# Hybrid neighbourhood-attention and short-convolution block: the two score banks of PSUM as two tiles outside the attention, and DRAM scratch split by head and pair

## The chip, the cores and the metric

The kernel runs on one core of one Trainium2 chip. Its time is the device time of one execution, in microseconds (us), lower is better. Five engines work side by side, each through its own instructions in order: TensorE (PE, with the weight loads listed apart as PEld), VectorE (DVE), ScalarE (ACT), GpSimd (POOL) and SyncE (SP, which here only issues DMAs). An engine waits on semaphores that other engines or DMA queues raise.

## The reference

One layer on a latent sequence of 1024 tokens (16 rows of 64), width 1024, with 256 context tokens. All arithmetic is in float32.

```
h  = rmsnorm(x, norm_g)   * (1 + scale)   + shift      # adaLN from silu(c) @ w_ada + b_ada
hc = rmsnorm(ctx, norm_g) * (1 + scale_c) + shift_c
q, k, v, za, u, bg, cg, zc = split(h @ w_in)           # each 512 wide
kc, vc = split(hc @ w_in[:, 512:1536])
q, k, kc = rmsnorm of each head (8 heads of 64)
s_lat = rope(q) . rope(k) * 64**-0.5 + rpb             # window of 8 x 16 of the grid
s_ctx = q . kc * 64**-0.5                              # all 256 context keys
attn  = softmax([s_lat, s_ctx]) @ [v, vc] * silu(za)
conv  = bg * conv3(cg * u) * silu(zc)
x_new = x + gate * (concat([attn, conv]) @ w_out)
```

## The kernel before

**Arithmetic.** To keep float32 accuracy every operand of a large product is split into a high part (rounded) and a low part (the rest): `wh`, `wl` for weights, `hh`, `hl` for the normalised input h, `qs`, `ks`, `vs` for q, k and v. A product is three matmuls, high x high, high x low and low x high (`mm3`). A split is a copy on ACT (the high part) and a subtraction on DVE (the low part), `halves` and `chunk_split` in the code.

**Stages.** By the span's time: the setup (modulation, norm, tables; to about 85 us), the projections of q, k and v (85 to 306), the attention (306 to about 640), and the output projection. In the setup and in the attention the order of instructions on each engine is the order of the program text (`strict`). In the projections and the output a scheduler of the compiler orders them by its own estimates of time.

**Projections.** A loop over n has 32 tiles, 4 pairs of heads with 8 tiles (t = 0 to 7) of 128 tokens each. `proj_tile` computes one tile's q, k and v of a pair: 8 steps k (128 rows of the weights each) of three matmuls with 384 columns, 24 matmuls into one bank of PSUM. In the same pass the loop works on the tiles before it:

- `head_scale`: ACT squares tile n-1 (`sq`), DVE sums by head (`ss`), POOL takes the power -1/2;
- `put_v`: ACT and DVE split v out of the bank (`vs`);
- `normed`: ACT scales q and k of tile n-2 (`qn`, four activations);
- `rotated`: DVE applies the rotary table (`rtmp`, `rot`);
- `turn_qk`: PE transposes two tiles (`trA`, `trB`), ACT and DVE split them (`qs`, `ks`), SP stores them to `q_d`, `k_d`;
- after tile 2 of a pair (tile 0 of the last pair) `ctx_products` makes the context's k and v in two banks `cacc` (48 matmuls); their `sq`, `kn`, `vs` and transposes (`trC`, two of them) follow one to three tiles later;
- in pair 1 the gate row of the modulation is summed by two matmuls (`pgate`) and copied by ACT (`gr`);
- in the first tiles and the last ones, units of the convolution and gates (`pu`) fill in; their weights are loaded as `uraw` and split into `uh`, `ul`.

The weights of the next pair are loaded in chunks (`wr`), 8 for a pair, and split into `wh` and `wl`, each of which has a ring of 12 buffers: the last four splits of a pair can start only when the running pair's matmuls have let go of the first buffers.

**PSUM.** It has 8 banks of [128, 512] float32. The pool `psm` has three tags with two buffers each: O, C and U. The tag S is something else, one tile `sbank` of two banks from which `bank` hands out the halves in turn:

```
    sbank = psm.tile([P, 2, 512], F32, name="pss")          # line 854
    ...
    def bank(name, tag):                                    # line 857
        if tag != "S":
            return psm.tile([P, 512], F32, name=name, tag=tag, bufs=2)
        turns[0] += 1
        return sbank[:, turns[0] % 2]
```

Tile t of a pair takes the bank `"OOSS"[t % 4]`: t = 0, 1, 4, 5 write O banks (named `pacc` in the profile), t = 2, 3, 6, 7 write S halves (named `pss`). In the attention PE writes two tiles of scores into the two halves, and DVE adds the bias to both in one instruction, so that there the two halves are read as one. The output projection takes S, C and O banks for its first six tiles, and then U and S in turn.

The compiler's framework (Tile) tracks who wrote and who read by tile: an instruction that reads a tile waits for the instructions ahead of it in the program that wrote that tile.

**DRAM scratch.** q, k, v and the context's kc and vc go through scratch in DRAM (`q_d`, `k_d`, `v_d`, `kc_d`, `vc_d`), one tensor each with the head as its first index. So do the tables of biases (`t4_d`), the sums of the softmax (`rs_d`, `ri_d`), the attention's output (`o_d`), the gates (`zs_d`) and their products (`y_d`).

**SP's queue.** SP issues nearly all transfers in one order: chunk loads, `uraw`, the stores (collected in `stores` and issued by `flush` a tile later), and at the end of the projections the first heads' loads of the attention, `k_s`, `q_s`, `kc_s` and `v` (`load_k`, `load_q`, `load_v`). A store waits in the queue until the engine that makes its data is done, and all behind it wait too.

Of the kernel before, what the change touches and what calls it, by code (L numbers as in the profile page):

```python
# [10 lines left out]
F32 = mybir.dt.float32  # L11
# [8 lines left out]
P = 128  # L20
D = 1024
T = 1024
L = 256
# [16 lines left out]
def body(tc, es, x, ctxt, w_ada, b_ada, w_in, q_g, k_g, rpbr, w_out, vecs, cst, out):  # L40
# [45 lines left out]


    dr = es.enter_context(tc.tile_pool(name="dr", bufs=1, space=DRAM))
    t2_d = dr.tile([8, NH * 31, 24], F32, name="t2_d")
    t3_d = dr.tile([NH, 16, 8, 384], F32, name="t3_d")  # L90
    t4_d = dr.tile([NH, P, 3 * 384], F32, name="t4_d")
    o_d = dr.tile([NPAIR, P, T], F32, name="o_d")
    y_d = dr.tile([KT, P, T], F32, name="y_d")
    g_d = dr.tile([1, D], F32, name="g_d")
    rope_d = dr.tile([P, 2048], F32, name="rope_d")
    rs_d = dr.tile([NH, 2, 512], F32, name="rs_d")
    zs_d = dr.tile([NPAIR, P, T], F32, name="zs_d")


    q_d = dr.tile([NH, 2, HD, 4, 2, 256], F32, name="q_d")  # L100
    k_d = dr.tile([NH, HD, 4, 2, 256], F32, name="k_d")
    v_d = dr.tile([NH, P, 4, 2, 2 * HD], F32, name="v_d")
    kc_d = dr.tile([NH, HD, 2, L], F32, name="kc_d")
    vc_d = dr.tile([NH, P, 2, 2 * HD], F32, name="vc_d")
    ri_d = dr.tile([NPAIR, 2, T], F32, name="ri_d")


    cp = es.enter_context(sbuf("cp"))
# [83 lines left out]
    def spill(dst, src):  # L192
        stores.append(lambda: sp.dma_start(dst, src.bitcast(F32)))
# [21 lines left out]
    def turn_qk(pp, p, two, t0):  # L215

        pA = psm.tile([P, 2, 2, P], F32, name="trA", tag="C", bufs=2)
        pB = psm.tile([P, 512], F32, name="trB", tag="C", bufs=2)
        for i, (qn, rot) in enumerate(two):
            pe.transpose(pA[:, 0, i], rot[:, 0:P], ident)  # L220
            pe.transpose(pA[:, 1, i], qn[:, 0:P], ident)
            pe.transpose(pB[:, i * P:(i + 1) * P], rot[:, P:256], ident)

        def put():
            qs = pp.tile([P, 2, 2, 256], F32R, name="qs", tag="qs", bufs=2)
            halves(qs[:, 0], qs[:, 1], pA[:].rearrange("p k i d -> p k (i d)"))
# [146 lines left out]
    def conv_group(i, done=None):  # L373
# [55 lines left out]
        def times(half, v, last):  # L429
            dve.tensor_tensor(by_row(cvs[half][:]), blocked(v), by_row(cvs[half][:]), ALU.mult)  # L430
            if last:
                sp.dma_start(y_d[4 + i, :, half * 512:(half + 1) * 512], cvs[half])

        def gains():
            for half, ps in sorted(done[CBG].items()) if done else ():
# [37 lines left out]
    def attn_group(f):  # L473

        z = []
        for got in unit(z_col(f)):
            if got:
                z.append(got)
            else:
                yield  # L480

        def on_act():
            for half, zs in enumerate(silus(z)):
                sp.dma_start(zs_d[f, :, half * 512:(half + 1) * 512], zs)
        chore(on_act)

    def recip(p, pl):

        ri = pl.tile([P, 16], F32, name="ri", tag="ri", bufs=2)
        pool.dma_start(ri, rs_d[2 * p:2 * p + 2].rearrange("h b (x c) -> (h b x) c", c=16))  # L490
        dve.reciprocal(ri, ri)
        pool.dma_start(ri_d[p].rearrange("h (x c) -> (h x) c", c=16), ri)

    def load_sums(f, half, rb, queue):
        for i in range(2):
            queue.dma_start(rb[64 * i:64 * i + 64],
                            ri_d[f, i:i + 1, half * 512:(half + 1) * 512].broadcast_to([64, 512]))


    prs = ExitStack()  # L500
# [41 lines left out]
    load_slab(1, 1)  # L542
    load_chunks([2, 3])
    load_slab(2, 0)

    pv = tr()
    pe.transpose(pv[:, :nvec], vec[:nvec], ident[:nvec, :nvec])
# [107 lines left out]
    acc0 = [{}, {}, {}]  # L655
    for u, half in (0, 0), (2, 0), (0, 1), (2, 1), (1, 0), (1, 1):
        acc0[u][half] = ps0.tile([P, 512], F32, name=f"acc{u}{half}", tag=f"acc{u}{half}")

    def first_columns(half, k, part=range(3)):

# [202 lines left out]
    uw = hs.enter_context(sbuf("uw", side="right"))  # L863

# [43 lines left out]
    class head:  # L908
# [13 lines left out]
        def load_q(self):  # L922
            h = self.h
            self.q = self.place().tile([P, 2, T], F32R, name="q_s", tag="B")
            self.kc = bmp.tile([P, 2, L], F32R, name="kc_s", tag="kc_s", bufs=2)
            for i in range(2):
                rows = slice(64 * i, 64 * i + 64)
                for k in range(2):
                    sp.dma_start(self.q[rows, k].bitcast(F32).rearrange("p (t c) -> p t c", c=256), q_d[h, i, :, :, k])
                sp.dma_start(self.kc[rows].bitcast(F32), kc_d[h])  # L930

        def load_v(self):
            h = self.h
            self.v = vts[h % 2]
            for l in range(2):
                for t in range(4):
                    sp.dma_start(self.v[:, l, 2 * t:2 * t + 2, 0:HD].bitcast(F32),
                                 v_d[h, :, t, l].rearrange("p (b d) -> p b d", d=HD))
                sp.dma_start(self.v[:, l, NB:, 0:HD].bitcast(F32), vc_d[h, :, l].rearrange("p (b d) -> p b d", d=HD))

        def masks(self):
            self.bt = bmp.tile([P, 3, 384], F32, name="bt", tag="bt", bufs=2)
# [67 lines left out]
        def finish(self, bank):  # L1010

            ob = ap.tile([P, 512], F32, name="ob", tag="ob", bufs=1)
            act.copy(ob[0:HD + 1], self.po[bank][0:HD + 1])
            act.dma_start(rs_d[self.h, bank:bank + 1], ob[64:65])
            act.dma_start(o_d[self.p, 64 * self.s:64 * self.s + 64, bank * 512:(bank + 1) * 512], ob[0:64])

    def pair_of(n):

# [123 lines left out]
    for n in range(NT + 3):  # L1142
# [42 lines left out]
        if 0 < n <= NT:  # L1185
            scales[n - 1] = head_scale(pp, tiles[n - 1], 4)
            if n % 2:
                vs = pp.tile([P, 2, 2, 2, HD], F32R, name="vs", tag="vs", bufs=4)
            put_v(vs, (n - 1) % 2, tiles[n - 1][:, 256:384])
            if n % 2 == 0:  # L1190
                q, r = divmod(n - 1, NB)
                for s in range(2):
                    spill(v_d[2 * q + s, :, r // 2], vs[:, s].rearrange("p l i d -> p l (i d)"))
        if t == at + 1 and n < NT:
            cscales = [head_scale(pp, a, 2) for a in cacc]

# [26 lines left out]
    flush()  # L1223
    pps.close()
    wps.close()


    vs_ = ExitStack()
# [8 lines left out]
    def gated(f):  # L1237

        ri = ap.tile([P, 16], F32, name="ri", tag="ri", bufs=2)
        sp.dma_start(ri, rs_d[2 * f:2 * f + 2].rearrange("h b (x c) -> (h b x) c", c=16))  # L1240
        yield
        dve.reciprocal(ri, ri)
        sp.dma_start(ri_d[f].rearrange("h (x c) -> (h x) c", c=16), ri)
        yield
        for half in range(2):
            cols = slice(half * 512, (half + 1) * 512)
            zs, tb, rb = (ap.tile([P, 512], F32, name=n, tag=n, bufs=1) for n in ("zs", "tb", "rb"))
            sp.dma_start(zs, zs_d[f, :, cols])
            sp.dma_start(tb, o_d[f, :, cols])
# [5 lines left out]
            sp.dma_start(y_d[f, :, cols], tb)  # L1255
# [32 lines left out]


    op = es.enter_context(sbuf("op"))  # L1290
    y, wo = {}, {}

    def load_wo(wp, nh, f):
# [8 lines left out]
    def put_y(yp, f):  # L1302
# [3 lines left out]
        for half in range(2):  # L1306
            cols = slice(half * 512, (half + 1) * 512)
            tb = op.tile([P, 512], F32, name="tb", tag="zt", bufs=4)
            if f == NPAIR - 1:
                zs = op.tile([P, 512], F32, name="zs", tag="zt", bufs=4)  # L1310
                rb = op.tile([P, 512], F32, name="rb", tag="rb", bufs=2)
                act.dma_start(zs, zs_d[f, :, cols])
                act.dma_start(tb, o_d[f, :, cols])
                load_sums(f, half, rb, pool)
                dve.tensor_tensor(zs, zs, rb, ALU.mult)
                dve.tensor_tensor(tb, tb, zs, ALU.mult)
            else:
                act.dma_start(tb, y_d[f, :, cols])
# [92 lines left out]
```

## Time and profile before

| What | Value |
|---|---|
| three runs | 685.97, 684.3, 685.97 us, median 685.97 |
| profiled execution | 682.2 us, span from first to last instruction 680.4 us |
| mean granted TensorE clock | 0.990 of full speed |
| busy, share of the span | PE 94%, PEld 80%, DVE 63%, ACT 47%, POOL 19% |
| DMA | 125.46 MB in 118864 packets, mean 184 GB/s |

Times in the views are us from the span's start. A row of the waits names the waiting engine and the destination of its instruction, the engine it waited for, the total in us, the number of waits and the longest. A row of the timeline gives start and length, engine, operation, destination and source, and in brackets the idle time of that engine just before it and what ended it. A row of the windows gives busy times of the engines with counts, the granted clock (PEclk) and the share of the DMA engines' time. Buffer numbers are left out of the names.

### The profile page before, as it was taken

The page shows a single profiled execution, that of the slowest core. Times are in us where ns is not written, and L with a number is a line of the kernel's source. Part 1 is how long each engine was busy: PE and PEld are TensorE (multiplying, and loading weights), DVE is VectorE, ACT ScalarE, POOL GpSimd, SP SyncE. Part 2 cuts the span into 40 slices and gives each one's busy share as a digit, 9 for nine tenths or more (in the row PEclk, how much of TensorE's full clock was granted, in tenths as well). Part 3 has the DMA queues.
Part 4 walks back from the last instruction along what each step waited for, and adds up shares of the span by engine and source line. Part 5 has one row for each costly group of instructions (what it writes and reads, how often), then busy time and mean ns, then how long its engine had stood idle before and what let it go on. Part 6 is the DMA issues. An engine that isn't in the chain of part 4 may idle for free.

```text
span 680.4 us, 10256 instructions
## 1 busy us (share of the span) xinstructions
PE 640.0 (94%) x3469; PEld 541.5 (80%) x3469; DVE 431.2 (63%) x814; ACT 321.6 (47%) x693; POOL 126.1 (19%) x137
## 2 busy tenths in 40 slices
PE   5899998999789888989999999999999999999997
PEld 1467798889689788968778788888888888888885
DVE  1566746683762754455879789987998874474211
ACT  3566725341451443343768656756576554352000
POOL 1105004112211222110111211111111111102521
PEclk9899999999999899999999999999999999999999
DMA  8873565755774879669977684969592232874721
GB/s 316 292 244 116 135 194 189 230 184 153 209 216 131 227 218 268 166 154 232 213 186 178 176 192 122 237 185 217 158 217 71 84 104 69 281 254 160 246 98 53
DMA packets 118864, 125.46 MB, mean 184 GB/s; under 512 B 32817, under 2 KB 89353, under 8 KB 117532
## 3 DMA queue, kind: packets, MB, share of 16 engines
q1 hardware_dynamic: 112348, 113.23, 59.9%
q10 hardware_dynamic: 6208, 11.05, 5.3%
q0 software_dynamic: 256, 0.54, 0.3%
q8 instruction: 27, 0.44, 0.3%
q14 instruction: 25, 0.20, 0.1%
HBM read 88.01 MB, written 38.53 MB: 186 GB/s over the span
## 4 chain that ended last, share of the span: by engine, by line
PE 61%; DVE 11%; DMA 9%; ACT 7%; SPq 6%; issue 4%; POOL 1%; ACTq 0%; DVEq 0%; POOLq 0%
PE pu L55 18%; PE pss L55 8%; PE po L55 5%; SPq L55 5%; PE pacc L55 5%; PE cacc L55 3%; PE tr L55 3%; PE pout L74 2%; PE pout L75 2%; PE pout L76 2%; PE pss L75 2%; PE pss L76 2%; PE pss L74 2%; PE pmx L55 2%; DMA k_s<-k_d 2%
## 5 line engine op out<-in xcount | busy, mean ns | idle before, releaser
L55 PE MATMUL pu<-h,uh 128*128 128x512 f32 x544 | 171.9, 397 | 1.1 <-DVE vs L55 1.1
L55 PEld LDWEIGHTS pu<-h,uh 128*128 128x128 f32 x544 | 98.7, 189 | 20.0 <-issue 1.3
L55 PE MATMUL pu<-h,ul 128*128 128x512 f32 x272 | 107.7, 396 | 0.0
L55 POOL TENSOR_TENSOR plc<-sc,phc 128x512 fp32r<-128x512 f32 x32 | 42.4, 1324 | 223.8 <-ACT sc L55 121.1
L55 PE MATMUL pacc<-wh,h 128*128 128x384 f32 x256 | 70.0, 345 | 2.1 <-ACT wh L55 2.1
L55 PE MATMUL pss<-wh,h 128*128 128x384 f32 x256 | 69.9, 345 | 0.0
L55 POOL TENSOR_TENSOR ss<-ss,mhalf 128x4 f32<-128x4 f32 (+1 forms) x40 | 38.8, 974 | 155.0 <-DVE ss L55 149.6
L55 PEld LDWEIGHTS pu<-h,ul 128*128 128x128 f32 x272 | 51.3, 189 | 12.4
L55 DVE TENSOR_REDUCE ss<-sq 128x4 f32<-128x260 f32 (+1 forms) x40 | 15.7, 393 | 68.7 <-ACT sq L55 67.7
L55 DVE TENSOR_TENSOR mx<-mx,sb 128x384 f32<-128x384 f32 (+1 forms) x64 | 55.1, 870 | 2.0
L55 PEld LDWEIGHTS pacc<-wh,h 128*128 128x128 f32 x256 | 47.7, 193 | 2.8 <-ACT wh L55 2.7
L55 PE MATMUL pacc<-wl,h 128*128 128x384 f32 x128 | 44.3, 346 | 3.9 <-DVE wl L55 3.9
L55 PEld LDWEIGHTS pss<-wh,h 128*128 128x128 f32 x256 | 47.6, 193 | 0.0
L55 PE MATMUL pss<-wl,h 128*128 128x384 f32 x128 | 43.7, 341 | 0.0
L55 ACT COPY mg<-pmx 128x256 f32<-128x256 f32 x32 | 12.0, 374 | 60.9 <-PE pmx L55 44.5
L55 ACT ACTIVATE sq<-pss 128x256 f32<-128x256 f32 x16 | 6.6, 414 | 68.9 <-PE pss L55 68.9
L55 DVE TENSOR_TENSOR pll<-sb,phl 128x768 fp32r<-128x768 f32 (+2 forms) x33 | 29.4, 889 | 7.9 <-ACT sb L55 7.9
L55 DVE TENSOR_TENSOR sc<-sc,mg 128x512 f32<-128x512 f32 x32 | 21.8, 682 | 18.2 <-ACT mg L55 18.2
L1344 POOL TENSOR_TENSOR ot<-ot,xr 128x512 f32<-128x512 f32 x15 | 20.0, 1347 | 68.7 <-DVE ot L1343 65.5
L55 PE MATMUL po<-phl,v 128*65 128x256 f32 (+2 forms) x160 | 31.2, 291 | 0.0
L55 DVE TENSOR_TENSOR sb<-pss,bt 128x768 f32<-128x768 f32 (+1 forms) x40 | 28.9, 737 | 3.0 <-PE pss L55 3.0
L55 PE MATMUL acc<-h,wh 128*128 128x512 f32 x96 | 29.6, 417 | 1.1 <-ACT wh L55 1.1
(161 smaller groups left out, 1430.5 us busy)
## 6 DMA issues: line engine op xcount, KB each, us to landing
uraw<-in_w_in SPq DMA_DIRECT2D x34, 256.0 KB
q_d<-qs SPq DMA_DIRECT2D x64, 128.0 KB
k_s<-k_d SPq DMA_DIRECT2D x16, 512.0 KB
q_s<-q_d SPq DMA_DIRECT2D x32, 256.0 KB
wr<-in_w_in SPq DMA_DIRECT2D x40, 192.0 KB
slab<-in_w_ada SPq DMA_DIRECT2D x6, 1024.0 KB
t_d<-btw SPq DMA_DIRECT2D x8, 576.0 KB
bt<-t_d SPq DMA_DIRECT2D x8, 576.0 KB
```

Source lines behind the costliest of these rows:

```text
L55: i = emit(*a, **kw)
L74: i = pe.matmul(ps, ah, bh, start=first, stop=False)
L75: pe.matmul(ps, ah, bl, start=False, stop=False)
L76: pe.matmul(ps, al, bh, start=False, stop=last)
L1344: (dve if (nh, t) == (1, NB - 1) else pool).tensor_tensor(ot, ot, xr, ALU.add)
```

## The change

In the projections and in the output the two S banks become two tiles of a pool of their own with a tag and two buffers. In the attention they are one double tile, from another pool opened there. The pool of the projections (`s_banks`) is closed ahead of the attention. The scratch tensors become lists with one tensor for each head or pair. The allocation of the setup's accumulators `acc0` is written further up.

```diff
     dr = es.enter_context(tc.tile_pool(name="dr", bufs=1, space=DRAM))
+
+    def many(name, n, shape):
+        return [dr.tile(shape, F32, name=f"{name}{i}")[:] for i in range(n)]
+
...
-    q_d = dr.tile([NH, 2, HD, 4, 2, 256], F32, name="q_d")
-    k_d = dr.tile([NH, HD, 4, 2, 256], F32, name="k_d")
-    v_d = dr.tile([NH, P, 4, 2, 2 * HD], F32, name="v_d")
-    kc_d = dr.tile([NH, HD, 2, L], F32, name="kc_d")
-    vc_d = dr.tile([NH, P, 2, 2 * HD], F32, name="vc_d")
+    q_d = many("q_d", NH, [2, HD, 4, 2, 256])
+    k_d = many("k_d", NH, [HD, 4, 2, 256])
+    v_d = many("v_d", NH, [P, 4, 2, 2 * HD])
+    kc_d = many("kc_d", NH, [HD, 2, L])
+    vc_d = many("vc_d", NH, [P, 2, 2 * HD])
...
-                    spill(q_d[h, l, :, t0 // 2], qs[rows, l])
-                spill(k_d[h, :, t0 // 2], ks[rows])
+                    spill(q_d[h][l, :, t0 // 2], qs[rows, l])
+                spill(k_d[h][:, t0 // 2], ks[rows])
...
     psm = es.enter_context(psum("psm"))
-    sbank = psm.tile([P, 2, 512], F32, name="pss")
-    turns = [0]
+
+    s_banks = ExitStack()
+    pss = s_banks.enter_context(psum("pss"))
 
     def bank(name, tag):
-        if tag != "S":
-            return psm.tile([P, 512], F32, name=name, tag=tag, bufs=2)
-        turns[0] += 1
-        return sbank[:, turns[0] % 2]
+        return (pss if tag == "S" else psm).tile([P, 512], F32, name=name, tag=tag, bufs=2)
...
     pps.close()
     wps.close()
+    s_banks.close()
...
-    with sbuf("att") as ap:
+    with sbuf("att") as ap, psum("psb") as psb:
+        sbank = psb.tile([P, 2, 512], F32, name="pss")
         strict[:] = every
...
     op = es.enter_context(sbuf("op"))
+    pss = es.enter_context(psum("pso"))
     y, wo = {}, {}
```

The other scratch tensors (`t4_d`, `o_d`, `y_d`, `rs_d`, `zs_d`, `ri_d`) are split in the same way. On DVE, ACT and POOL the instructions and their order are the same before and after; on PE three matmuls of the output projection change places; on SP eight transfers move.

On ACT the change is in what instructions wait for. This is ACT in pair 2, before: `sq` and `vs` of an S tile, the squares of the two `cacc` banks, `qn` of the O tile ahead of them, the splits of the transposed q and k, and then `sq` of the second S tile and `qn` of the first. The names' numbers tell the buffers apart, and in brackets stand the engines and queues that an instruction waits for.

```order
L55 ACTIVATE sq_898<-pss_891 128x4x64 [waits DVE_49,PE_49]
L55 CAST vs_2346<-pss_891 128x2x64 [waits DMAHW7_49,DMAHW6_49]
L55 ACTIVATE sq_898<-cacc_2253 128x2x64 [waits DVE_49]
L55 ACTIVATE sq_898<-cacc_2254 128x2x64 [waits DVE_49]
L55 ACTIVATE qn_2357<-pacc_2152,ss_2234 128x64 [waits Pool_49]
...
L55 CAST qs_2362<-trA_2303 128x512 [waits DMAHW5_49,DMAHW6_49,DMAHW1_49,DMAHW0_49]
...
L55 ACTIVATE sq_898<-pss_891 128x4x64 [waits DVE_49]
...
L55 ACTIVATE qn_2413<-pss_891,ss_2343 128x64 [waits DVE_49,Pool_49]
```

The first `sq` waits for PE up to the last write of the whole tile `pss_891`, and what follows has no further wait for PE. The same place after:

```order
L55 ACTIVATE sq_961<-pacc_2280 128x4x64 [waits DVE_49,PE_49]
L55 CAST vs_2419<-pacc_2280 128x2x64 [waits DMAHW7_49,DMAHW6_49]
L55 ACTIVATE sq_961<-cacc_2325 128x2x64 [waits DVE_49,PE_49]
L55 ACTIVATE sq_961<-cacc_2326 128x2x64 [waits DVE_49,PE_49]
L55 ACTIVATE qn_2430<-pacc_2223,ss_2306 128x64 [waits PE_49,Pool_49]
...
L55 CAST qs_2435<-trA_2375 128x512 [waits DMAHW5_49,DMAHW1_49,DMAHW6_49,DMAHW0_49,PE_49]
...
L55 ACTIVATE sq_961<-pacc_2390 128x4x64 [waits DVE_49,PE_49]
...
L55 ACTIVATE qn_2486<-pacc_2280,ss_2416 128x64 [waits Pool_49]
```

No row has moved. The two S tiles now have two names (`pacc_2280`, `pacc_2390`), each `sq` waits for PE up to its own tile, the squares of `cacc` and the splits have waits for PE of their own, and `qn` waits for DVE no more.

On SP the places of transfers change at the end of the projections. Before, where the last tiles' q, k and v are stored, the values `v` of the first head (some of them) and the weights `uraw` of a filling unit are loaded:

```order
L55 DMA v_d<-vs 128x256 x2
L937 DMA v_3346<-v_d 128x2x64 x4
L55 DMA q_d<-qs 64x512
L939 DMA v_3346<-vc_d 128x2x64
L55 DMA q_d<-qs 64x512
L55 DMA k_d<-ks 64x512
L55 DMA q_d<-qs 64x512 x2
L55 DMA k_d<-ks 64x512
L55 DMA uraw<-in_w_in 128x4x128 x2
L55 DMA v_d<-vs 128x256 x2
L937 DMA v_3346<-v_d 128x2x64 x4
L939 DMA v_3346<-vc_d 128x2x64
```

After, with the head's number in the scratch's name, from the last two stores of v on:

```order
L55 DMA v_d_112<-vs 128x256
L939 DMA v_3426<-v_d_105 128x2x64 x4
L941 DMA v_3426<-vc_d_121 128x2x64
L939 DMA v_3426<-v_d_105 128x2x64 x3
...
L939 DMA v_3426<-v_d_105 128x2x64
...
L55 DMA q_d_96<-qs 64x512 x2
L55 DMA k_d_104<-ks 64x512
L941 DMA v_3426<-vc_d_121 128x2x64
L288 DMA uraw<-in_w_in 128x4x128 x2
```

The loads of v have moved behind the last stores of v and in part behind stores of q and k, the last one to just ahead of a load of `uraw`.

More of the change, by code (lines that the diff above doesn't have):

```diff
@@ L88, in body @@
     dr = es.enter_context(tc.tile_pool(name="dr", bufs=1, space=DRAM))
+    def many(name, n, shape):
+        return [dr.tile(shape, F32, name=f"{name}{i}")[:] for i in range(n)]
     t2_d = dr.tile([8, NH * 31, 24], F32, name="t2_d")
     t3_d = dr.tile([NH, 16, 8, 384], F32, name="t3_d")
-    t4_d = dr.tile([NH, P, 3 * 384], F32, name="t4_d")
-    o_d = dr.tile([NPAIR, P, T], F32, name="o_d")
-    y_d = dr.tile([KT, P, T], F32, name="y_d")
+    t4_d = many("t4_d", NH, [P, 3 * 384])
+    o_d = many("o_d", NPAIR, [P, T])
+    y_d = many("y_d", KT, [P, T])
     g_d = dr.tile([1, D], F32, name="g_d")
     rope_d = dr.tile([P, 2048], F32, name="rope_d")
-    rs_d = dr.tile([NH, 2, 512], F32, name="rs_d")
-    zs_d = dr.tile([NPAIR, P, T], F32, name="zs_d")
-    q_d = dr.tile([NH, 2, HD, 4, 2, 256], F32, name="q_d")
-    k_d = dr.tile([NH, HD, 4, 2, 256], F32, name="k_d")
-    v_d = dr.tile([NH, P, 4, 2, 2 * HD], F32, name="v_d")
-    kc_d = dr.tile([NH, HD, 2, L], F32, name="kc_d")
-    vc_d = dr.tile([NH, P, 2, 2 * HD], F32, name="vc_d")
-    ri_d = dr.tile([NPAIR, 2, T], F32, name="ri_d")
+    rs_d = many("rs_d", NPAIR, [2, 2, 512])
+    zs_d = many("zs_d", NPAIR, [P, T])
+    q_d = many("q_d", NH, [2, HD, 4, 2, 256])
[3 more added lines that the diff above has]
+    vc_d = many("vc_d", NH, [P, 2, 2 * HD])
+    ri_d = many("ri_d", NPAIR, [2, T])
     cp = es.enter_context(sbuf("cp"))
@@ L431, in times @@
             if last:
-                sp.dma_start(y_d[4 + i, :, half * 512:(half + 1) * 512], cvs[half])
+                sp.dma_start(y_d[4 + i][:, half * 512:(half + 1) * 512], cvs[half])
         def gains():
@@ L483, in on_act @@
             for half, zs in enumerate(silus(z)):
-                sp.dma_start(zs_d[f, :, half * 512:(half + 1) * 512], zs)
+                sp.dma_start(zs_d[f][:, half * 512:(half + 1) * 512], zs)
         chore(on_act)
@@ L489, in recip @@
         ri = pl.tile([P, 16], F32, name="ri", tag="ri", bufs=2)
-        pool.dma_start(ri, rs_d[2 * p:2 * p + 2].rearrange("h b (x c) -> (h b x) c", c=16))
+        pool.dma_start(ri, rs_d[p].rearrange("h b (x c) -> (h b x) c", c=16))
         dve.reciprocal(ri, ri)
@@ L496, in load_sums @@
             queue.dma_start(rb[64 * i:64 * i + 64],
-                            ri_d[f, i:i + 1, half * 512:(half + 1) * 512].broadcast_to([64, 512]))
+                            ri_d[f][i:i + 1, half * 512:(half + 1) * 512].broadcast_to([64, 512]))
     prs = ExitStack()
@@ L544, in body @@
     load_slab(2, 0)
+    acc0 = [{}, {}, {}]
+    for u, half in (0, 0), (2, 0), (0, 1), (2, 1), (1, 0), (1, 1):
+        acc0[u][half] = ps0.tile([P, 512], F32, name=f"acc{u}{half}", tag=f"acc{u}{half}")
     pv = tr()
@@ L653, in turn_ctx @@
             modulated(hc[k // 4][:, k % 4, 0], hc[k // 4][:, k % 4, 1], pts[k2][:, kk * 256:(kk + 1) * 256], k, 1, (act, dve)[kk])
-    acc0 = [{}, {}, {}]
-    for u, half in (0, 0), (2, 0), (0, 1), (2, 1), (1, 0), (1, 1):
-        acc0[u][half] = ps0.tile([P, 512], F32, name=f"acc{u}{half}", tag=f"acc{u}{half}")
     def first_columns(half, k, part=range(3)):
@@ L928, in load_q @@
                 for k in range(2):
-                    sp.dma_start(self.q[rows, k].bitcast(F32).rearrange("p (t c) -> p t c", c=256), q_d[h, i, :, :, k])
+                    sp.dma_start(self.q[rows, k].bitcast(F32).rearrange("p (t c) -> p t c", c=256), q_d[h][i, :, :, k])
                 sp.dma_start(self.kc[rows].bitcast(F32), kc_d[h])
@@ L937, in load_v @@
                     sp.dma_start(self.v[:, l, 2 * t:2 * t + 2, 0:HD].bitcast(F32),
-                                 v_d[h, :, t, l].rearrange("p (b d) -> p b d", d=HD))
-                sp.dma_start(self.v[:, l, NB:, 0:HD].bitcast(F32), vc_d[h, :, l].rearrange("p (b d) -> p b d", d=HD))
+                                 v_d[h][:, t, l].rearrange("p (b d) -> p b d", d=HD))
+                sp.dma_start(self.v[:, l, NB:, 0:HD].bitcast(F32), vc_d[h][:, l].rearrange("p (b d) -> p b d", d=HD))
         def masks(self):
@@ L1013, in finish @@
             act.copy(ob[0:HD + 1], self.po[bank][0:HD + 1])
-            act.dma_start(rs_d[self.h, bank:bank + 1], ob[64:65])
-            act.dma_start(o_d[self.p, 64 * self.s:64 * self.s + 64, bank * 512:(bank + 1) * 512], ob[0:64])
+            act.dma_start(rs_d[self.p][self.s, bank:bank + 1], ob[64:65])
+            act.dma_start(o_d[self.p][64 * self.s:64 * self.s + 64, bank * 512:(bank + 1) * 512], ob[0:64])
     def pair_of(n):
@@ L1192, in body @@
                 for s in range(2):
-                    spill(v_d[2 * q + s, :, r // 2], vs[:, s].rearrange("p l i d -> p l (i d)"))
+                    spill(v_d[2 * q + s][:, r // 2], vs[:, s].rearrange("p l i d -> p l (i d)"))
         if t == at + 1 and n < NT:
@@ L1239, in gated @@
         ri = ap.tile([P, 16], F32, name="ri", tag="ri", bufs=2)
-        sp.dma_start(ri, rs_d[2 * f:2 * f + 2].rearrange("h b (x c) -> (h b x) c", c=16))
+        sp.dma_start(ri, rs_d[f].rearrange("h b (x c) -> (h b x) c", c=16))
         yield
@@ L1247, in gated @@
             zs, tb, rb = (ap.tile([P, 512], F32, name=n, tag=n, bufs=1) for n in ("zs", "tb", "rb"))
-            sp.dma_start(zs, zs_d[f, :, cols])
-            sp.dma_start(tb, o_d[f, :, cols])
+            sp.dma_start(zs, zs_d[f][:, cols])
+            sp.dma_start(tb, o_d[f][:, cols])
             load_sums(f, half, rb, sp)
@@ L1254, in gated @@
             dve.tensor_tensor(tb, tb, zs, ALU.mult)
-            sp.dma_start(y_d[f, :, cols], tb)
-    with sbuf("att") as ap:
+            sp.dma_start(y_d[f][:, cols], tb)
+    with sbuf("att") as ap, psum("psb") as psb:
+        sbank = psb.tile([P, 2, 512], F32, name="pss")
         strict[:] = every
@@ L1311, in put_y @@
                 rb = op.tile([P, 512], F32, name="rb", tag="rb", bufs=2)
-                act.dma_start(zs, zs_d[f, :, cols])
-                act.dma_start(tb, o_d[f, :, cols])
+                act.dma_start(zs, zs_d[f][:, cols])
+                act.dma_start(tb, o_d[f][:, cols])
                 load_sums(f, half, rb, pool)
@@ L1317, in put_y @@
             else:
-                act.dma_start(tb, y_d[f, :, cols])
+                act.dma_start(tb, y_d[f][:, cols])
             tv = blocked(tb[:]) if f < NPAIR else by_row(tb[:])
```

## The prediction

> **What bounds the kernel now.** I read the page's head first, then the busy time by stage, then what TensorE waits for in the stage that has idle time, then what holds the engine behind that wait.
>
> ```profile
> span 680.4 us, 10256 instructions
> PE 640.0 (94%) x3469; PEld 541.5 (80%) x3469; DVE 431.2 (63%) x814; ACT 321.6 (47%) x693; POOL 126.1 (19%) x137
> ...
> core 0: us, PE busy (x) PEld busy (x) DVE busy (x) ACT busy (x) POOL busy (x), PEclk, DMA share, GB/s
> 85.30:306.00 220.70, 199.82 (x1168) 187.94 (x1167) 124.56 (x332) 83.28 (x303) 44.91 (x53) 0.98 0.68 195
> 306.00:400.00 94.00, 90.54 (x493) 74.33 (x494) 69.66 (x107) 60.04 (x96) 14.77 (x13) 0.98 0.82 192
> 400.00:650.00 250.00, 249.87 (x1317) 208.29 (x1316) 184.10 (x281) 127.48 (x210) 46.02 (x42) 1.00 0.62 172
> ```
>
> TensorE (PE) is the bound: 640.0 of 680.4 us. Of its 40.4 us of idle time, 220.70 - 199.82 = 20.9 us lie in the projections (85.3 to 306), 3.5 in the first third of the attention, 0.1 in the rest up to 650. So only the projections have something to win, and the waits there say what:
>
> ```profile
> PE trC L55 <- DVE qs L55: 8.4, 3, 3.2
> PE pacc L55 <- DVE wl L55: 3.9, 5, 1.4
> PE trA L55 <- DVE rot L55: 3.7, 4, 1.2
> PE pacc L55 <- ACT wh L55: 2.1, 2, 1.1
> PE pc L55 <- DVE qs L55: 1.1, 1, 1.1
> PE pu L55 <- DVE vs L55: 1.1, 1, 1.1
> PE trA L55 <- DVE qs L55: 0.7, 1, 0.7
> ...
> ACT sq L55 <- PE pss L55: 68.9, 8, 13.4
> ACT qn L55 <- DVE vs L55: 20.2, 8, 3.8
> ```
>
> The columns are total us, times, longest. The PE rows add to 21.0 us in 17 waits, all of it for late work of VectorE (DVE) and ScalarE (ACT), which are busy only 56% and 38% of this stage. They are late because ACT itself stands: 68.9 us in 8 waits of sq for pss. There are eight couples of S tiles (t = 2,3 and 6,7 of four pairs), so it is one wait a couple. Pair 2 shows it; first PE's chain (start, length), then ACT:
>
> ```profile
> 202.13 4.16 PE pss L55 x24
> 206.29 5.76 PE cacc L55 x48
> 212.71 4.17 PE pss L55 x24
> ...
> 216.90 0.39 ACT L55 ACTIVATE sq<-pss 128x256 f32<-128x256 f32 x1 [13.37 <-PE pss L55]
> ```
>
> The first S tile is complete at 202.13 + 4.16 = 206.3, the second at 216.9, and sq of the first starts at 216.90. ACT reads tile 2 only when tile 3 is complete, 10.6 us too late where the context products lie between, one tile (4.2 us) where they don't. ACT runs in order, so all that stands behind sq is as late.
>
> **The change, part by part.** *Two tiles for sbank in the projections.* No instruction is added or removed. The wait of sq, and of DVE's vs, ends with its own tile; so does that of qn for vs (20.2 us), which now names its own tile's vs. What becomes of PE's 17 waits:
>
> ```profile
> 222.43 0.33 PE L55 MATMUL trA<-ci,rot 128*128 128x128 f32 x1 [0.81 <-DVE rot L55]
> ```
>
> trA of pair 2 waits until rot is done at 222.4. Started at 206.3 instead of 216.9, the chain is next held by cacc (206.29 + 5.76 = 212.05), 4.8 us before 216.9; rot is then done near 217.6, and PE asks at 221.6. Cover 4 us: cost zero. The two trC waits of pairs 2 and 3, the seven for wh and wl at the pair ends and pu's go the same way, each 1.4 us long at most or, of trC, no more than 3.2, against a shift of 4.2 or more. At the pair ends a bound comes behind: the ring of 12 wh. The last four splits wait until tile 7's own matmuls have used steps 0 to 3, half of its 4.17 us; that leaves 2 us for casts and subtractions that I put at some 0.5 each (ACT's sq takes 0.39; ACT and DVE work side by side). I take zero, and keep this term as a rival.
>
> Three waits stay:
>
> ```profile
> 102.59 0.62 ACT L55 CAST uh<-uraw 128x512 fp32r<-128x512 f32 x1 [12.27 <-DMA uraw<-in_w_in]
> 107.95 0.39 ACT L55 ACTIVATE sq<-pss 128x256 f32<-128x256 f32 x1 [0.46 <-PE pss L55]
> 113.61 0.33 PE L55 MATMUL trA<-ci,rot 128*128 128x128 f32 x1 [1.20 <-DVE rot L55]
> 180.62 0.41 PE L55 MATMUL trC<-ci,kn 128*128 128x128 f32 x2 [3.16 <-DVE qs L55]
> 305.98 1.22 PE L55 MATMUL pc<-q_s,kc_s 128*128 128x256 f32 x4 [1.05 <-DVE qs L55]
> ```
>
> In pair 0 ACT is late by a weight load (12.27 us), and sq gains 0.46 us at most: 1.20 stays. In pair 1 the gate's row sum (pgate) stands between PE's tile and trC, and ACT's copies of it stand ahead of qs: 3.16 stays. pc needs a C bank that DVE's last qs has to read first, straight behind the last transposes: 1.05 stays. The last two waits of trA (0.7, and one of the two that share the remaining 3.7 - 1.20 - 0.81 = 1.7, some 0.85) come from SP:
>
> ```profile
> 296.25 1.20 SPq L55 DMA_DIRECT2D uraw<-in_w_in  x2
> ...
> 299.91 0.62 ACT L55 CAST uh<-uraw 128x512 fp32r<-128x512 f32 x1 [4.12 <-DMA uraw<-in_w_in]
> ```
>
> SP's stores of q ahead of this load stand until ACT's qs, which is behind a late sq, and ACT then waits 4.12 us for the load. One tile earlier (4.2), it has landed: both waits go.
>
> So 14 waits go: 21.0 - 1.20 - 3.16 - 1.05 = 15.6 us. Each also costs a restart that idle time doesn't show:
>
> ```profile
> L55 PE MATMUL pacc<-wh,h 128*128 128x384 f32 x256 | 70.0, 345 | 2.1 <-ACT wh L55 2.1
> ```
>
> One matmul lasts 345 ns, but 24 in a row take 4.16 us, 173 ns each, so every stop loses 0.17 us of overlap: 14 x 0.17 = 2.4 us.
>
> *The clock.* Three slices show a granted clock of 0.83, each behind a stop:
>
> ```profile
> 230.00:240.00 10.00, 10.00 (x53) 9.97 (x52) 5.32 (x16) 1.39 (x6) 1.01 (x1) 0.83 0.89 261
> 270.00:280.00 10.00, 9.83 (x51) 9.83 (x52) 5.70 (x19) 4.36 (x16) 2.02 (x2) 0.83 0.80 225
> 300.00:310.00 10.00, 7.41 (x30) 5.55 (x29) 5.54 (x13) 5.05 (x13) 0.00 (x0) 0.83 0.81 210
> ...
> 143.03 2.80 PE pu L55 x12
> 230.02 5.72 PE pss L55 x24
> 236.39 4.18 PE pss L55 x24
> 270.58 5.73 PE pacc L55 x24
> 307.20 3.74 PE pu L55 x12
> ```
>
> The first two cost 5.72 - 4.18 = 1.54 and 5.73 - 4.18 = 1.55 us, the third 3.74 - 2.80 = 0.94 and some of pc before it: 4.0 to 4.6, I take 4.4. The stops ahead of them are trC of pairs 2 and 3 and the cluster at 302 to 306, of which only pc's remains. But the stop of 3.16 us in pair 1, which was followed by none, may meet one the next time: I take off half of 1.55, 0.8. [...]
>
> *DRAM scratch by head and pair.* As many transfers of the same sizes. SP's order moves in two places: the load of head 1's context keys goes behind four stores, and of head 0's values (v0) some pieces go behind stores of the last projection tiles, the last of them to just ahead of the next weight load.
>
> ```profile
> 309.89 0.60 SPq L55 DMA_DIRECT2D k_d<-ks  x1
> ...
> 322.85 0.48 PE L55 MATMUL po<-phc,v 128*65 128x256 f32 x2
> ...
> 337.62 10.94 DMA v<-v_d
> ```
>
> That last piece would now start behind the store at 309.89, at 310.5; PE needs it at 322.85. Even the 10.94 us of the slowest v load on the chain end at 321.4. Zero, with 1.4 us of cover at the worst; gone, it would cost a few us once. The context keys are needed two quarters of an attention head later still: zero.
>
> *The attention's double tile and the output's two tiles.* The attention keeps one tile written and read as a whole. In the output the wait of ot for its neighbour goes, but PE is busy 249.87 of 250 us there: zero. acc0's allocation moves without an instruction.
>
> Sum: 15.6 + 2.4 + 4.4 - 0.8 = 21.6 us. The profiled execution took 682.2 us (span 680.4 and 1.8 around it), so 660.6 by its own time; the median of the three runs is 685.97, 0.55% more, and gives 664.4. I say 664.
>
> **The rivals.** *A: the next wait takes over* (ring of wh, VectorE's order). Then the seven pair-end waits stay, 3.9 + 2.1 + 7 x 0.17 = 7.2 us: 672. For it: the ring's slack is only 2 us. Against: DVE is busy 56%.
>
> *B: the gain is given back at the start of the attention.* From 306 to 400 the DMA share is 0.82, and the attention's first loads lie there. If they end at the same time as now, what pair 3 and the tail win (half of trC's other 5.2, trA's 0.7 and 0.85, three restarts, dips of 1.55 and 1.3: 2.6 + 1.55 + 0.5 + 2.85 = 7.5) turns into waits for them: 664 + 7.5, some 672. Against: PE idles only 3.5 us there now, and SP's stream moves earlier with ACT.
>
> *C: nothing happens*, because something other than S holds ACT and DVE: 686. The trace's 68.9 us against one releaser speak against it. [...]
>
> *D: slower.* Each head's scratch lies elsewhere in DRAM, and its strided loads could get slower. The place is 306 to 400, DMA share 0.82: at a factor f the transfers need 94 x 0.82 x f us there. The gain of 21.6 is eaten once 77.1 f > 94 + 21.6, f > 1.50; at 1.6 it is 686 + 7.8 = 694. Nothing in the trace speaks for it, and nothing shows the new places.
>
> **How the numbers follow.** Main case 0.74, 660 to 668 (clock dips all gone or all kept, pair 0's wait gone too). A 0.11, B 0.08, C 0.04, D 0.03. A change under 0.3% (2 us) can't be told from none. The range goes from 658 (all 17 waits and restarts but pc's, all dips: 20 + 2.7 + 4.6 = 27) to 674, which takes in A and B and leaves out C and D. Faster 0.93, same 0.04, slower 0.03.
>
> **What would show it.** ACT's row sq <- PE pss should be gone, and its waits for pacc stay a few us each; PE's waits in the projections fall from 21.0 to about 5.4, with trC of pair 1 the longest; the attention's first scores come some 21 us earlier; PEclk 0.83 at one place or none. Wrong if wl or wh still end PE's waits at the pair ends (A), if po or pss wait for v or k_s at the attention's start (B), or if DMA rows of k_s and v get longer (D).

## The result and the profile after

The changed kernel takes 661.6 us (median of four runs, 660.23 to 665.69) against 685.97 us: a ratio of 0.9659 of the mean times, with a 95% interval of 0.9614 to 0.9705. Here and below medians and ratios leave out slow executions: one of 690.12 us with the banks in the order O S O S, and one of 2210 us with the gate row's matmuls a tile later. Forecast were 664 us and a range of 658 to 674. The profiled execution took 661.21 us, 21.0 us less than the profiled one before. Its page's head, then by the windows the stretch from the first projection tile to the first context scores (198.6 us; the same work took 85.34 to 305.98, 220.6 us, before), then TensorE's waits in it:

```profile
span 659.4 us, 10276 instructions
PE 635.2 (96%) x3469; PEld 539.5 (82%) x3469; DVE 432.2 (66%) x814; ACT 322.8 (49%) x693; POOL 129.1 (20%) x137
```

```profile
core 0: us, PE busy (x) PEld busy (x) DVE busy (x) ACT busy (x) POOL busy (x), PEclk, DMA share, GB/s
87.80:286.40 198.60, 192.88 (x1167) 185.29 (x1165) 125.01 (x332) 84.27 (x303) 48.08 (x53) 1.00 0.76 219
286.40:374.40 88.00, 84.08 (x469) 69.19 (x470) 65.55 (x101) 56.77 (x92) 13.50 (x12) 1.00 0.81 190
```

```profile
PE trC L55 <- DVE qs L55: 3.2, 1, 3.2
PE trA L55 <- DVE rot L55: 1.4, 1, 1.4
PE pc L55 <- DVE qs L55: 1.1, 1, 1.1
```

TensorE's idle time in the stage is 198.60 - 192.88 = 5.7 us, where it was 20.9, and its seventeen waits are three: those that the prediction left standing. The reason shows on ScalarE. These are its rows in pair 2, the place of the prediction's first timeline:

```profile
202.01 0.39 ACT L55 ACTIVATE sq<-pacc 128x256 f32<-128x256 f32 x1 [2.79 <-PE pacc L55]
202.29 0.26 ACT L55 CAST vs<-pacc 128x128 fp32r<-128x128 f32 x1
207.42 0.28 ACT L55 ACTIVATE sq<-cacc 128x128 f32<-128x128 f32 x1 [4.87 <-PE cacc L55]
...
209.14 0.62 ACT L55 CAST qs<-trA 128x512 fp32r<-128x512 f32 x1
...
212.59 0.39 ACT L55 ACTIVATE sq<-pacc 128x256 f32<-128x256 f32 x1 [2.56 <-PE pacc L55]
...
216.55 0.27 PE L55 MATMUL trA<-ci,rot 128*128 128x128 f32 x1
```

sq of the first S tile starts at 202.01, as TensorE begins the context products, and that of the second a good ten us later at its own tile's end. Before, both started behind the second tile, 10.6 us too late for the first. The transposes trA at 216.55 wait for nothing. In the profile as a whole sq now has 51.7 us of waits for 23 tiles, 3.2 us at most, where it had 68.9 us in eight for S tiles and 9.3 in four for O tiles.

### The profile page after: what moved, and what is told of

Its sections match the earlier page's. It is cut to its first block, busy times and chain, and to the rows that moved or that the text cites. A ratio compares the mean times of both kernels' runs of the same rounds, so it can differ in the third digit from the quotient of the medians.

```text
span 659.4 us, 10276 instructions
## 1 busy us (share of the span) xinstructions
PE 635.2 (96%) x3469; PEld 539.5 (82%) x3469; DVE 432.2 (66%) x814; ACT 322.8 (49%) x693; POOL 129.1 (20%) x137
## 4 chain that ended last, share of the span: by engine, by line
PE 66%; DMA 10%; DVE 10%; ACT 5%; SPq 4%; issue 2%; POOL 1%; ACTq 0%; DVEq 0%; POOLq 0%
PE pu L55 18%; PE pacc L55 17%; PE pout L74 4%; PE pout L76 4%; PE pout L75 4%; PE po L55 4%; SPq L55 3%; PE tr L55 3%; PE cacc L55 3%; DVE mx L55 2%; DMA uraw<-in_w_in 2%; DVE sb L55 2%; DMA k_s<-k_d 2%; DMA v<-v_d 2%; PE pss L55 2%
## 5 line engine op out<-in xcount | busy, mean ns | idle before, releaser
L55 PE MATMUL pacc<-wh,h 128*128 128x384 f32 x512 | 135.5, 339 | 0.1
L55 PEld LDWEIGHTS pacc<-wh,h 128*128 128x128 f32 x512 | 92.9, 188 | 0.5 <-ACT qn L55 0.4
L55 PE MATMUL pacc<-wl,h 128*128 128x384 f32 x256 | 86.0, 336 | 0.0
L75 PE MATMUL pout<-wol,yh 128*128 128x512 f32 x128 | 50.1, 391 | 0.0
L76 PE MATMUL pout<-woh,yl 128*128 128x512 f32 x128 | 50.0, 392 | 0.0
L74 PE MATMUL pout<-woh,yh 128*128 128x512 f32 x128 | 48.7, 392 | 0.0
L55 PEld LDWEIGHTS pacc<-wl,h 128*128 128x128 f32 x256 | 48.2, 188 | 0.1
L55 ACT ACTIVATE sq<-pacc 128x256 f32<-128x256 f32 x32 | 12.4, 387 | 52.6 <-PE pacc L55 51.7
L1348 DVE TENSOR_TENSOR ot<-pout,gate 128x512 f32<-128x512 f32 x16 | 10.8, 688 | 40.3 <-PE pout L76 38.1
L1349 POOL TENSOR_TENSOR ot<-ot,xr 128x512 f32<-128x512 f32 x15 | 19.6, 1316 | 70.0 <-DVE ot L1348 68.9
L55 ACT ACTIVATE qn<-pacc,ss 128x64 f32<-128x64 f32 x128 | 30.1, 329 | 6.5 <-POOL ss L55 3.2
```

Source lines behind the costliest of these rows:

```text
L55: i = emit(*a, **kw)
L74: i = pe.matmul(ps, ah, bh, start=first, stop=False)
L75: pe.matmul(ps, ah, bl, start=False, stop=False)
L76: pe.matmul(ps, al, bh, start=False, stop=last)
L1348: dve.tensor_tensor(ot, ps, gate[:, cols], ALU.mult)
L1349: (dve if (nh, t) == (1, NB - 1) else pool).tensor_tensor(ot, ot, xr, ALU.add)
```

## The experiments

All ratios are to the kernel before, timed beside each kernel.

**The two S tiles alone.** The diff's parts for `bank`, `s_banks`, `psb` and `pso`; scratch and acc0 as before.

> The kernel before with the two S banks as two tiles (projections, output) and the double tile in the attention alone; the DRAM scratch and acc0 stay as they were. Theory S (all of the gain comes from the waits of sq, vs and qn for the neighbour's tile): as fast as the changed kernel, 661.6 us within 3 us, the row of ACT's sq waiting for a whole double tile gone, TensorE's waits in the projections about 5.7 us as after. Rival R (the split scratch and the new places of SP's transfers bring the gain): near 686 us. Rival M (each brings a part): between 666 and 682 us.

666.8 us, ratio 0.971 (0.9682 to 0.9739): most of the gain, so rival R is out, but 5 us short of Theory S and just inside the range of rival M. Up to the first output of the attention TensorE was 20.3 us ahead of the kernel before, as in the changed kernel (21.0). Then ScalarE stood (its rows and one of TensorE in the timeline, and a slice of the windows, whose granted clock is the 0.77 behind the five busy times):

```profile
324.08 0.56 ACT L55 COPY ob<-po 65x512 f32<-65x512 f32 x1
...
328.78 0.49 ACTq L1012 DMA_DIRECT2D rs_d<-ob  x1
331.11 0.53 ACTq L1013 DMA_DIRECT2D o_d<-ob  x1
331.74 0.37 ACT L55 COPY mg<-pmx 128x256 f32<-128x256 f32 x1 [4.70 <-DMA v<-v_d]
...
335.44 0.98 PE L55 MATMUL pmx<-ci,mx 128*128 128x128 f32 x2 [2.32 <-DVE mx L55]
```

```profile
330.00:340.00 10.00, 7.39 (x30) 5.67 (x29) 5.93 (x10) 4.93 (x8) 1.69 (x1) 0.77 0.55 138
```

The stores of the finished output (ob) are issued from ScalarE's own row. By the trace's semaphore events each stood for an earlier load of SP's whose end raises the same semaphore as its own: the first was issued at 328.78, when a load of k_s had landed at 328.70, the second at 331.11, when a load of v had landed at 331.09. What was queued behind them made DVE's mx late, TensorE stopped for 2.3 us, and a half clock followed (0.77 in that slice).

This kernel has one more stop, which neither of the two kernels compared has, where TensorE begins the first projection tile:

```profile
90.35 0.44 PE L55 MATMUL pacc<-wh,h 128*128 128x384 f32 x1 [2.27 <-DVE hw L55]
```

VectorE makes hw at the setup's end from transposes that lie in PSUM. With the old scratch and the old place of acc0, every profile below in which the S tiles are apart, or in which the first tile takes an S half, has this stop of 2.3 us; with the split scratch and the moved acc0 none of two S tiles has it. A bank of PSUM can come free late for acc0's place, hardly for the scratch, which lies in DRAM, so by my reading this points to acc0; no run here separates the two. TensorE begins 2.5 us later than in the changed kernel, of which 0.6 are left at the first context scores.

**The scratch alone.** The changed kernel with the one double tile everywhere.

> The changed kernel with the old S banks: one double tile everywhere; only the scratch lists and the moved acc0 stay. Theory S: no gain, 686 us within 2 us, ACT's sq again waits 69 us in 8 waits. Rival R: 662 us. Rival M: what it wins here is missing from the run with the banks alone, between 666 and 682 us.

688.23 us, ratio 1.0026 (1.0002 to 1.0049): no gain, and sq waits for pss again, 70.8 us in eight waits. Theory S holds for the scratch with the moved acc0. Its profile has a wait of 2.1 us of the first tile for ScalarE's ub, which the kernel before hasn't, so a small gain of the scratch could be hidden by it.

**Another order of the banks, the double tile kept.** `bank("pacc", "OSOS"[t % 4])` in place of `"OOSS"`.

> The kernel before with its double tile, but the banks of the projection tiles in the order O S O S in place of O O S S; nothing else. When sq of an S tile is emitted, the next tile's matmuls then write an O bank, so sq no longer waits for a neighbour; qn of an S tile, which is emitted two tiles later, does. Theory S (what counts is which instruction waits for a second tile, and sq stands too early for it): most of the gain comes without any new tile, 661 to 669 us, sq's waits for pss short, qn's longer. Rival L (the gain comes from two separate tiles as such, for instance from how the two banks lie or are shared): no gain, 683 to 688 us. A result of 670 to 682 us would say that qn's wait for the neighbour costs nearly as much as sq's.

685.19 us, ratio 0.998 (0.9945 to 1.0014): nothing. Theory S failed here in the form that I had given it. sq was early, as it said, but ScalarE's row shows another instruction at the same place:

```profile
202.76 0.26 ACT L55 CAST vs<-pacc 128x128 fp32r<-128x128 f32 x1
207.35 0.93 ACT L55 ACTIVATE qn<-pss,ss 128x64 f32<-128x64 f32 x4 [4.33 <-issue]
...
217.91 0.28 ACT L55 ACTIVATE sq<-cacc 128x128 f32<-128x128 f32 x1 [0.76 <-PE trB L55]
222.10 0.93 ACT L55 ACTIVATE qn<-pss,ss 128x64 f32<-128x64 f32 x4 [3.91 <-PE pss L55]
222.90 0.61 ACT L55 CAST qs<-trA 128x512 fp32r<-128x512 f32 x1
```

qn of an S tile is emitted two tiles later, when the neighbour is already written in the program. It stands until that tile ends, and qs behind it is as late as before. TensorE's waits in the stage were 18.9 us in 14 (21.0 in 17 before). Two of them, 4.2 us, are a cost of this order itself: matmuls into one half wait for DVE's vs, which before never held them up. I had asked which instruction waits; what counts is when ScalarE gets past it.

**An order in which nothing waits, the double tile kept.** `bank("pacc", "SOO"[n % 3])`, n counting all tiles.

> The kernel before with its double tile, scratch and all, but the banks of the projection tiles in the order S O O S O O over all 32 tiles in place of O O S S. When the last reader of an S half (qn, two tiles later) is emitted, the next S tile isn't written yet: no instruction of ACT or DVE then waits for a neighbour, and the waits on ACT are those of the changed kernel, with one tile for both halves. Theory S2 (after the O S O S order gave nothing: what counts is that no instruction in ACT's row stands for a neighbour's matmuls, whichever it is): the gain comes without any new tile, 661 to 668 us, TensorE's waits in the projections 5 to 8 us. Rival L (the two tiles as such bring it): 683 to 688 us. Rival W (the S half is taken again after three tiles in place of four, and matmuls wait for qn and vs of the tile before in it): 670 to 680 us, with waits of pss for ACT or DVE of 0.5 us or more a tile.

667.37 us, ratio 0.9725 (0.969 to 0.976). One tile, the old scratch, and no instruction on ScalarE that stands for a neighbour: this is within 0.6 us of the two S tiles alone in their first runs, 3.0 us from their 664.39 us beside it on the same chip, and 18.7 us faster than before. So two tiles as such are not what helps (rival L), or at most for those 3 us. Rival W has a small share: one wait of pss for qn, 1.6 us.

**The double tile in pairs 0 and 1 only.** The changed kernel with `sbank` handed out for the first eight S tiles.

> The changed kernel, but with the double tile in pairs 0 and 1 of the projections; pairs 2 and 3 and the output have two tiles. Theory S with local waits (each pair pays for its own late sq): the first two pairs' share of the gain is lost. In the two traces TensorE is 4.3 us ahead at pair 2's second tile and 2.5 us behind at the projections' start, so 6.8 us: 661.6 + 6.8 = 668.4 us, within 2.5 us. Rival Q (lateness builds up from pair to pair, so that the late pairs' long stops are the early pairs' doing): the late pairs stop as before, 676 us or more. Rival Q2 (the early pairs cost nothing, only the late ones with their clock dips do): 662 us within 2 us.

669.35 us, ratio 0.9745 (0.9724 to 0.9766), where 668.4 was expected. Each pair pays for its own late sq; Q and Q2 are out.

**The changed kernel and the two S tiles beside each other.**

> The changed kernel unchanged, beside the others on one chip. Its four times so far had mean granted clocks of 0.986 to 0.995 and lay at 660.2 to 665.7 us, the kernel before at 0.980 to 0.988 in 19 runs and at 683.7 to 690.4. A mean clock c means (1 - c) x 2 x span of half clock: 10 us in the changed kernel, 22 us before. If the clock is a part of the gain, as the sum had it, the mean clock of these runs is 0.990 or more and the median 660 to 664 us; if it was luck, the clocks of both kernels meet near 0.986 and the median is 664 to 667 us.

> The two S tiles alone, without the split scratch, beside the changed kernel on one chip. It had 666.8 us before, with TensorE as far ahead as in the changed kernel (20.3 against 21.0 us) up to 331 us, and then a stop of 2.3 us and a half clock of 6.8 us in the attention, where ACT's store of the first output stands for a load of v. Theory S (the scratch brings nothing; that stop is a matter of when the transfers land in one execution or another): the same as the changed kernel within 2 us. Rival P (the split scratch makes the transfers at the attention's start land earlier, and that is worth something only when the projections are short): 3 to 6 us slower than the changed kernel, mean clock below 0.990 in most runs.

661.06 us (0.9647, 0.9611 to 0.9682) and 664.39 us (0.9675, 0.9641 to 0.9709). With the earlier runs that is ten of each, 662.2 and 665.1 us in the mean (standard deviations 2.6 and 2.5), so the split scratch and the moved acc0 together are worth some 3 us, give or take 2.4, once the S tiles are apart. Rival P's time is met; its clock is not, since four of the six runs of the two S tiles have 0.991 or more. The stop of 2.27 us at the first tile is a part of the difference: by the first context scores 0.6 of it was left in the first profile of the two S tiles. Mean clocks: 0.9911 over ten runs of the changed kernel, 0.9839 over 40 of the kernel before. The traces of the two kernels compared record a granted clock of 1.00 or 0.50 and nothing between (before, 0.50 in the windows from 230.70 to 234.00 us and 1.00 from 234.10 to 271.50), so (1 - c) x 2 x span, with c the mean clock, = 11.8 and 22.1 us at half clock. The clock is a part of the gain.

**The gate row's matmuls one tile later.** `if n == KT + 6: gate.sum()`.

> The changed kernel with the two matmuls of the gate row (pgate) and their copies (gr) one tile later in pair 1, behind the tile at whose end trC stands. Theory (trC's remaining stop of 3.2 us is ACT standing for pgate ahead of qs): the stop goes, 3.2 us and a restart of 0.2, so 3.4 us faster than the changed kernel, TensorE's waits in the projections 2 to 3 us. Rival (ACT stands for pgate one tile later just as long, and the next trA or the pair's end pays for it): no change within 1.5 us.

661.7 us, ratio 0.9634 (0.9606 to 0.9662). trC's stop is gone, but the rival is right:

```profile
181.30 0.33 PE L55 MATMUL trB<-ci,rot 128*128 128x128 f32 x1 [2.22 <-DVE ks L55]
```

**ScalarE's copies of the gate row later, the matmuls in place.** `sum` keeps the two matmuls; the copies are appended to `waiting` behind `turn_kc`.

> The changed kernel; pgate's two matmuls stay where they are, but ACT's two copies of them (gr) stand behind the next tile's sq, qn and the splits of q and k instead of ahead of them. TensorE's order is unchanged. Theory (trC's last stop is ACT standing for pgate, and moving the matmuls a tile later only moved the stop to trB): the 3.2 us stop and its restart go, 3.4 us, and with it the half clocks that began at that stop in six of nine profiles (3.4 or 6.8 us long, so 1.7 to 3.4 us each, some 1.5 in the mean): median 655 to 658.5 us, mean clock 0.991 or more. Rival (something else of ACT or DVE is late there too): trC or the trA after it waits 2 us or more, 660 to 662 us.

657.49 us, ratio 0.9598 (0.9573 to 0.9623), as expected, though the interval just overlaps that of the changed kernel. TensorE's order is the changed kernel's, and the stop is gone. First the changed kernel's timeline, then this one's and a slice of its windows:

```profile
174.40 1.88 PE L55 MATMUL pgate<-gacc,ones 128*1 128x512 f32 x4
179.44 0.41 PE L55 MATMUL trC<-ci,kn 128*128 128x128 f32 x2 [3.17 <-DVE qs L55]
```

```profile
173.04 1.88 PE L55 MATMUL pgate<-gacc,ones 128*1 128x512 f32 x4
174.84 0.44 PE L55 MATMUL trC<-ci,kn 128*128 128x128 f32 x2
```

```profile
180.00:190.00 10.00, 10.00 (x62) 9.97 (x62) 8.94 (x25) 6.57 (x25) 3.18 (x3) 1.00 0.82 253
```

From pgate to trC it was 5.04 us, now 1.80.

**And ob's stores from GpSimd's queue.** `pool.dma_start` in place of `act.dma_start` in `finish`.

> The same, and the attention's stores of ob (rs_d and o_d, 32 transfers) issued from GpSimd's queue instead of ACT's. Theory (at the attention's start ACT stands 2 to 5 us at the first of these stores until an earlier load of SP's has landed, DVE's mx is late behind it, and TensorE stops 2 to 4.7 us in small pieces, with a half clock in three of eight profiles): 1.5 to 4 us faster than the run with the gate copy alone, ACT's waits for v and k_s gone. Rival (the stores cost GpSimd time ahead of plc, for which po waits): po's waits for plc grow and it is slower by 1 us or more. Rival (the loads themselves are late, and something else waits for them): no change within 1.5 us.

655.18 us, ratio 0.9563 (0.954 to 0.9585): another 2.3 us by the medians, though the two intervals just overlap. pmx's waits for mx from 285 to 400 us fell from 2.3 to 1.1 us, and no wait of po for plc came up. How the stores bring it is shown only in part: the two profiled executions differ by 2.1 us, of which 1.3 lie between the first context scores and the output's first matmul, and in the profile without this edit ScalarE stood only 1.0 us at the first stores. This is the fastest version.

**The same with the old scratch.**

> The fastest version so far (two S tiles, gr behind, ob's stores from GpSimd's queue; 655.2 us, ratio to the kernel before 0.9563) with the scratch of the kernel before, one tensor each. In ten runs each the S tiles with the split scratch took 662.2 us in the mean and with the old one 665.1. Theory T (the old scratch is slower only through ACT's stores, which stand for the loads): with the stores off ACT's queue nothing is left, ratio 0.954 to 0.9585, 655 us within 1.5. Rival P (the old scratch's loads or SP's order are slower for something else too): 657 to 659 us, ratio 0.959 or more.

655.97 us, ratio 0.9564 (0.9539 to 0.9589): with ob's stores off ScalarE's queue the old scratch costs nothing that these runs can tell, even with the stop of 2.27 us at the first tile, of which 1.0 us was left at the first context scores and nothing at the output's first matmul. Theory T holds: most of what the split scratch was worth, it was worth through those stores. The loads that they stand for took 11.0 to 13.1 us from issue to landing in the two profiles of the two S tiles alone and 8.6 to 11.9 in those of the changed kernel. Why was not found: SP's transfers have the same order in both.

**Rings of 10.** `bufs=10` for wh and wl in the changed kernel.

> The changed kernel with rings of 10 buffers for wh and wl in place of 12. This prices the term that the prediction took as zero: with 12 the last four splits of a pair wait for steps 0 to 3 of the pair's last tile (2 us left), with 10 the last six for steps 0 to 5 (1 us left). Theory A (the ring is the next bound and 2 us is just enough): waits of pacc for wh or wl come back at the three pair ends, 0.5 to 1.5 us each, and with restarts and half clocks it is 2 to 7 us slower than the changed kernel. Rival (1 us is enough too): the same within 1.5 us. Rival H (ACT, in order, stands at the early splits for the last tile, and sq, qn and the transposes behind it are late): trA waits too, 7 us slower or more.

667.83 us, ratio 0.9753 (0.9727 to 0.978), 6.8 us slower than the changed kernel's 661.06: the upper end of Theory A.

```profile
PE pacc L55 <- DVE wl L55: 2.5, 4, 0.9
...
PE trA L55 <- DVE rot L55: 1.4, 1, 1.4
```

The waits for wl are back, and trA waits no more than in the changed kernel, so rival H is out. From the first tile to the first context scores it takes 204.3 us, 5.7 more than the first profile of the changed kernel, and some 1.55 of that is a half clock at pair 1's stop, such as the changed kernel has in its second profile. At the attention's start ScalarE stood 4.3 us for v and 3.7 for k_s; the changed kernel has such waits too (3.9 for k_s in its second profile), so that they come from the ring is not shown.

## Why the prediction was right, step by step

- **The bound and the mechanism.** Right. ScalarE and VectorE stood for a neighbour's matmuls; the order S O O shows that ending those waits brings most of the gain (18.7 of 25.0 us beside the changed kernel), O S O S that moving them on the same engine does not.
- **Which waits go.** 15.6 us forecast, 21.0 - 5.7 = 15.3 measured. The three that were to stay are the three that stayed, trA of pair 0 at 1.4 instead of 1.2. The waits of trA at the end are gone too, but not because the load has landed when ScalarE asks for it. ScalarE still waits 3.05 us for it, where it waited 4.12:

```profile
277.11 0.62 ACT L55 CAST uh<-uraw 128x512 fp32r<-128x512 f32 x1 [3.05 <-DMA uraw<-in_w_in]
```

  What helps is that this is 7.2 us ahead of the last transposes, at 284.33; before, the cast began at 299.91, 2.0 us ahead of the time at which TensorE asked for them.
- **The ring of wh (rival A).** With 12 buffers no wait for wh or wl is left, as forecast, and with 10 they are back: the 2 us of slack are real, and there is not much more than that, as waits of up to 0.9 us come with two buffers less.
- **Restarts.** 2.4 us forecast. From the first tile to the first scores the gain is 220.6 - 198.6 = 22.0 us; less 15.3 of idle time and two half clocks of 1.55, 3.6 are left, 0.26 for each of the fourteen if nothing else is in it.
- **The clock.** Too small. The three dips of the profiled execution are gone, as forecast (the granted clock is 1.00 from 87.80 to 374.40 us). But over 40 runs the kernel before spends 22.1 us at half clock, not the 13.7 of its profiled execution, so 10.3 us of half clock go; at 1.55 for 3.41 that is an estimate of 4.7 us against the 3.6 in the sum. The profiled execution of before had less half clock than most of its runs. The 0.8 taken off for pair 1's stop was right in kind: the next profile of the changed kernel has a half clock there, and the run with ScalarE's copies later, 657.49 against 661.06 us, shows what the stop and its half clocks cost together.
- **The sum.** 22.0 in the projections, 1.5 more at the attention's start, where the third dip was, less 2.5 in the setup, where the profiled execution of the changed kernel had 10.2 us of half clock by the trace's record of the clock and that of before 3.4. One of its slices in the setup:

```profile
20.00:30.00 10.00, 8.12 (x22) 5.77 (x23) 7.03 (x15) 5.08 (x9) 2.56 (x4) 0.67 1.10 338
```

  That makes 21.0, as the two profiled executions differ, and setup and dips are not the same from run to run; the medians differ by 24.4.
- **DRAM scratch and acc0: zero.** Right beside the double tile (1.0026), wrong beside the S tiles by some 3 us for both together. The step that failed looked for cover only at TensorE's need of v (1.4 us for the last piece). What in fact stands for the loads is ScalarE at its own stores of ob, for 4.70 us up to 331.74 in the profile of the tiles alone. The moved order of SP, which the prediction put down to the scratch, is not the scratch's: with the scratch alone SP issues its transfers as before, with the two S tiles alone as in the changed kernel. And acc0's move, taken as nothing, most likely spares the two S tiles the stop of 2.27 us at the first projection tile.
- **Rival B** (the gain given back at the attention's start) is thereby true in part: by other waits than the ones I named, and for some 2 us by the medians with the stores on GpSimd's queue. In the worst profile, the first of the two S tiles alone, TensorE's lead falls from 20.3 us at the first po to 14.6 at the output's first matmul.
- **Attention and output: zero.** Right: TensorE is 21.0 us ahead at the first pmx and 20.9 at the first matmul of the output (587.33 before; the attention's matmuls end by then and not near 640, as the stages above have it).

## What to carry to other kernels

Under this framework a PSUM tile is waited for as a whole: where halves of one tile are written in turn, every reader of the first half that is emitted behind the second's matmuls stands for both (here sq, for 68.9 us in eight waits), and on an in-order engine all that is queued behind it is as late (in the order O S O S qs, at 222.90 behind qn at 222.10). Look for it where a wait of a slack engine is longer than the tile it reads took to write, and ask when the engine gets past the place, not which instruction waits there. Once the stops are out, look at the stores that a busy engine issues itself: here they stood for loads that have nothing to do with its work, for 4.70 us up to 331.74 with the two S tiles alone.

## What the hardware showed that was not expected

A stop of 3.2 us was followed by a half clock in some profiles here, not in all. Ten profiles here have the same stop of 3.2 us in pair 1; in seven a half clock of 3.41 or 6.83 us begins during it or within 2 us of its end, by the trace's record of the clock, in three (the two kernels compared and the first run of the S tiles alone) none. The four kernels whose longest stop in the projections is 2.3 us or less have none there. The changed kernel, in the profile taken beside the two S tiles, in the timeline and the windows:

```profile
178.41 0.66 PE L55 MATMUL trC<-ci,kn 128*128 128x128 f32 x2 [3.17 <-DVE qs L55]
```

```profile
170.00:180.00 10.00, 6.83 (x30) 4.99 (x29) 3.29 (x10) 5.30 (x19) 1.01 (x1) 0.87 0.36 107
180.00:190.00 10.00, 10.00 (x51) 9.97 (x50) 7.22 (x22) 4.30 (x14) 2.01 (x2) 0.79 0.89 272
```

TensorE reads as busy through the whole of the second slice, at a clock of 0.79. From pgate to the next context products it took 2.6 us longer than in the first profile of the same kernel. So with its half clock a stop of 3.2 us cost 5.8, and which of the two it is changes from run to run: the ten times of the changed kernel range over 7.4 us, the six of the kernel with the copies behind over 3.1.
